# Layer 0's MLP of a two-layer decoder kernel: two stages over both halves of the tokens in place of one pass per half

## The chip, the cores and the metric

The kernel runs on one core of one Trainium2 chip, alone. The metric is device time in microseconds (us) of one execution; lower is better. TensorE (PE in the profile) multiplies, VectorE (DVE), ScalarE (ACT) and GpSimd (POOL) work on tiles of 128 partitions, and SyncE (SP) issues all DMAs between DRAM and SBUF from one queue, in program order. Each engine runs its own instructions in the order in which the program lists them. TensorE writes PSUM, which has here two wide buffers (pS, 1024 floats a partition) and four narrow ones (pB, 512).

## What is computed

A trunk of two decoder layers over 1024 tokens with 1024 features. Layer 0 has an attention over keys that an indexer selects (top 256 of the earlier ones), layer 1 a sliding window; both also read a fixed memory. Behind each attention stands a gated MLP with a causal convolution over three tokens. Cut to what matters here:

```python
D_MODEL, SEQ, DEPTH, D_FF, CONV_WIDTH = 1024, 1024, 2, 2816, 3

def conv_glu_ffn(h, w_up, conv_w, conv_b, w_down):
    S = h.shape[1]
    a, b = jnp.split(h @ w_up, 2, axis=-1)
    a_pad = jnp.pad(a, ((0, 0), (CONV_WIDTH - 1, 0), (0, 0)))
    a = sum(conv_w[j] * a_pad[:, j:j + S] for j in range(CONV_WIDTH)) + conv_b
    return (jax.nn.silu(a) * b) @ w_down

for i in range(DEPTH):
    h = rmsnorm(x, g_mix[i])
    mix, q_mem = mixer_a(h, ...) if i == 0 else mixer_b(h, ...)
    mem_o = memory_cross_attention(q_mem, mem_n, w_mem_kv[i])
    x = x + jnp.concatenate([mix, mem_o], axis=-1) @ w_out
    x = x + conv_glu_ffn(rmsnorm(x, g_ffn[i]), f_w_up[i], f_conv_w[i], f_conv_b[i], f_w_down[i])
return rmsnorm(x, g_final)
```

rmsnorm divides each token by the root of its mean square and multiplies each feature by a gain.

## The kernel before

**Tiles.** Activations lie with features on partitions and tokens along the row. Tokens are worked in two halves of 512 (`HT`). A half of x or h is four tiles, called pairs here, of 128 partitions x 1024: two blocks of 128 features, 512 tokens each. The 2816 inner features of the MLP are 22 tiles f of 128.

**Products.** Each fp32 operand is split into a rounded high part and a remainder, and `mm3` (L253) issues three matmuls for one product: high x high (L256), high x low (L257), low x high (L258). `proj` (L530) makes one tile of a projection by 8 blocks x 3 = 24 matmuls. `Weights` brings weights in the order of use: `LOAD` = 5 units are loaded ahead (512 KB each), `SPLIT` = 2 are split ahead: ScalarE casts the high part (L99) and POOL subtracts the remainder in two pieces of 512 (`rest`, L272, L279).

**What sets the order.** The program is written straight down for TensorE, and `tick(ns)` moves a clock by what the matmuls issued so far should take. Work beside it is written as generators (`add_bg`): each yields the time until its next step and is advanced by `tick`, at a rate of its own. So the place of each step among the instructions of VectorE, ScalarE and POOL is fixed when the program is built. Stores to DRAM are put off by 4000 ns of that clock, and a load from the same place flushes them first.

**Layer 0's MLP.** `run` (L1718) goes through the two halves: attention of the half (`run_a`), then `ffn` (L789) for that half alone. The attention's output step makes x; `prepare` takes its squares and splits x times gain without the scale of the norm, the raw h. `scale_of` sums the squares (folded on VectorE, L404 and L412, then summed by TensorE, L424), and spreads the scale as rb (transposes on TensorE, L443, a copy by ScalarE, L445). In `ffn`, `up(f)` projects raw h to the two parts a and b of tile f, `conv` multiplies a by rb (L801), does the convolution's middle tap on ScalarE (L802) and two more on VectorE (L803, L804), then Silu (L810) and the product with rb on POOL (L811); `gate` multiplies by b (L816) and splits the result (L820, POOL). After each two tiles `down` adds one chunk of the down projection of the chunk before to x (8 outputs in pairs, 48 matmuls into pS, four sums on VectorE, L867). Up and down weights are loaded once for each half.

**Beside it.** The selection of the 256 keys for the blocks 4 to 7 of 128 queries (`topk`, L1229) is a binary search over 32 bits: in each bit ScalarE counts by signs for blocks 6 and 7 (L1274), VectorE by comparisons for blocks 4 and 5 (L1254), and VectorE moves the candidates (L1265, L1267). It is held during the output step of half 0's attention (`late[1] = 0.0`), and goes on beside half 0's MLP once rb is there (`topk_on`), a step for each 2400 ns of the clock at rate 1.056. Then it builds the masks, and `begin_a` starts the second attention. Memory attention for half 1 follows in `memory`. Beside half 1's MLP run half 0's norm for layer 1 (`norm0`) and the memory's norm, keys and values (`mem_kv`).

**Layer 1's MLP** is built otherwise. `ffn_up` makes normalized h of both halves (`norm_apply`, L450: two products on VectorE for a pair, L469, a high part by ScalarE, L480, and a remainder on VectorE for pairs 0 and 2, L461, on POOL for the others), projects three tiles in the usual way, and the other 19 by seven products of blocks in place of eight (`group`), whose right factors are sums and differences of h blocks (`right_factors`, L892) and whose left factors come from `Weights._factor`. The gated results go to DRAM (`G_d`), and `ffn_down` reads them back chunk by chunk for both halves, with the down weights loaded once.

## Time and profile before

| | us |
|---|---|
| median of 3 runs (2630.15 to 2631.1) | 2630.22 |
| the profiled execution | 2624.22 |
| its span in the trace | 2622.4 |

The profile is one execution, so durations and sums are made against 2624.22 and then set against the median. By the page the engines were busy for 94% (TensorE), 65% (VectorE), 53% (POOL) and 46% (ScalarE) of the span. A busy TensorE is not TensorE at its peak: a matmul's records overlap the next one's, so the number of matmuls in a stretch without a gap is the better price. The stages lie, by the lines that end them, at: inputs of layer 0 to about 307 us, first attention to 530, half 0's MLP to 939, second attention to 1118, half 1's MLP to 1511, layer 1's attention to 1905, its up stage to 2353, its down stage to 2605.

### The profile page before, as it was taken

The page shows a single profiled execution, that of the slowest core. Times are in us where ns is not written, and L with a number is a line of the kernel's source. Part 1 is how long each engine was busy: PE and PEld are TensorE (multiplying, and loading weights), DVE is VectorE, ACT ScalarE, POOL GpSimd, SP SyncE. Part 2 cuts the span into 40 slices and gives each one's busy share as a digit, 9 for nine tenths or more (in the row PEclk, how much of TensorE's full clock was granted, in tenths as well). Part 3 has the DMA queues.
Part 4 walks back from the last instruction along what each step waited for, and adds up shares of the span by engine and source line. Part 5 has one row for each costly group of instructions (what it writes and reads, how often), then busy time and mean ns, then how long its engine had stood idle before and what let it go on. Part 6 is the DMA issues. An engine that isn't in the chain of part 4 may idle for free. (4 is left out here: it accounts for less than half of the span.)

```text
span 2622.4 us, 34006 instructions
## 1 busy us (share of the span) xinstructions
PE 2457.8 (94%) x11912; PEld 2053.0 (78%) x11912; DVE 1708.0 (65%) x2961; ACT 1207.9 (46%) x2270; POOL 1387.8 (53%) x1241
## 2 busy tenths in 40 slices
PE   7789978989998999999999989999989999999997
PEld 5678856878886888877888878878767888888886
DVE  7787788877688466665653353498786556564446
ACT  5355666655542555433333334588644444442003
POOL 5644223456665633365766665566656666664204
PEclk9899999999998999999999999999989999999999
DMA  5453343423322343322333345642254232348401
GB/s 202 148 172 120 127 159 135 149 78 97 98 87 91 126 155 107 113 97 82 105 127 97 99 115 187 213 139 88 81 193 137 104 122 97 123 170 329 142 16 65
DMA packets 121083, 333.83 MB, mean 127 GB/s; under 512 B 13008, under 2 KB 29904, under 8 KB 120912
## 3 DMA queue, kind: packets, MB, share of 16 engines
q1 hardware_dynamic: 120912, 331.66, 37.4%
q8 instruction: 94, 1.54, 0.2%
q14 instruction: 77, 0.63, 0.1%
HBM read 258.21 MB, written 73.40 MB: 126 GB/s over the span
## 5 line engine op out<-in xcount | busy, mean ns | idle before, releaser
L279 POOL TENSOR_TENSOR t<-t,t 128x512 fp32r<-128x512 f32 x829 | 1108.2, 1368 | 681.0 <-ACT t L99 273.6
L256 PE MATMUL pB<-t,t 128*128 128x512 f32 (+3 forms) x1824 | 682.1, 374 | 11.9 <-DVE t L781 4.1
L257 PE MATMUL pB<-t,t 128*128 128x512 f32 (+3 forms) x1824 | 678.8, 372 | 5.0 <-DVE t L461 2.4
L258 PE MATMUL pB<-t,t 128*128 128x512 f32 (+3 forms) x1824 | 678.3, 372 | 5.4 <-POOL t L279 5.4
L256 PE MATMUL pS<-t,t 128*128 128x512 f32 (+1 forms) x1460 | 573.8, 393 | 40.0 <-ACT t L99 19.1
L258 PE MATMUL pS<-t,t 128*128 128x512 f32 (+1 forms) x1460 | 568.5, 389 | 8.0 <-POOL t L279 7.8
L257 PE MATMUL pS<-t,t 128*128 128x512 f32 (+1 forms) x1460 | 568.0, 389 | 2.1 <-DVE t L512 2.1
L256 PEld LDWEIGHTS pB<-t,t 128*128 128x128 f32 (+1 forms) x1824 | 346.2, 190 | 72.8 <-DVE t L781 4.7
L258 PEld LDWEIGHTS pB<-t,t 128*128 128x128 f32 (+1 forms) x1824 | 345.9, 190 | 66.7 <-POOL t L279 6.7
L257 PEld LDWEIGHTS pB<-t,t 128*128 128x128 f32 (+1 forms) x1824 | 346.2, 190 | 64.7 <-DVE t L461 3.3
L256 PEld LDWEIGHTS pS<-t,t 128*128 128x128 f32 x1460 | 281.7, 193 | 100.4 <-ACT t L99 22.8
L99 ACT CAST t<-t 128x1024 fp32r<-128x1024 f32 x284 | 288.0, 1043 | 101.5 <-PE pS L258 44.1
L258 PEld LDWEIGHTS pS<-t,t 128*128 128x128 f32 x1460 | 281.0, 192 | 67.4 <-POOL t L279 12.1
L257 PEld LDWEIGHTS pS<-t,t 128*128 128x128 f32 x1460 | 281.8, 193 | 53.2 <-DVE t L512 2.5
L265 DVE TENSOR_TENSOR t<-pB,t 128x512 fp32r<-128x512 f32 (+3 forms) x248 | 149.8, 623 | 85.3 <-ACT t L264 82.7
L264 ACT CAST t<-pB 128x512 fp32r<-128x512 f32 (+3 forms) x248 | 125.7, 534 | 158.1 <-PE pB L258 96.2
L1055 DVE TENSOR_TENSOR t<-t,pS 128x1024 f32<-128x1024 f32 (+1 forms) x92 | 107.9, 1174 | 125.6 <-PE pS L258 125.5
L811 POOL TENSOR_TENSOR t<-t,t 128x512 f32<-128x512 f32 x44 | 57.5, 1306 | 161.6 <-ACT t L810 161.6
L867 DVE TENSOR_TENSOR t<-t,pS 128x1024 f32<-128x1024 f32 x88 | 106.8, 1217 | 53.0 <-PE pS L258 52.7
L1274 ACT ACTIVATE sign<-t,ti 128x1024 bf16<-128x1024 f32 (+1 forms) x96 | 96.5, 1005 | 60.5 <-DVE ti L1267 49.1
L1447 POOL TENSOR_SCALAR t<-t,st 128x128 f32<-128x128 f32 (+3 forms) x64 | 47.9, 750 | 141.3 <-DVE st L1446 88.0
L1222 DVE SCALAR_TENSOR_TENSOR t<-t,wtok,t 128x384 f32<-128x384 f32 (+5 forms) x90 | 97.0, 1077 | 24.5 <-ACT t L1217 20.7
(228 smaller groups left out, 3027.6 us busy)
## 6 DMA issues: line engine op xcount, KB each, us to landing
t<-in_up SPq DMA_DIRECT2D x138, 512.0 KB
t<-in_down SPq DMA_DIRECT2D x66, 512.0 KB
G_d<-t SPq DMA_DIRECT2D x44, 512.0 KB
t<-G_d SPq DMA_DIRECT2D x44, 512.0 KB
t<-in_a_in SPq DMA_DIRECT2D x34, 512.0 KB
t<-in_b_in SPq DMA_DIRECT2D x28, 512.0 KB
t<-in_a_out SPq DMA_DIRECT2D x20, 512.0 KB
t<-x_d SPq DMA_DIRECT2D x20, 512.0 KB
```

Source lines behind the costliest of these rows:

```text
L99: nc.scalar.copy(hi[:, :w], raw[:, :w])
L256: mm(out, a[0], b[0], start=start, stop=False, skip_group_check=again)
L257: mm(out, a[0], b[1], start=False, stop=False, skip_group_check=again)
L258: mm(out, a[1], b[0], start=False, stop=stop, skip_group_check=again)
L264: nc.scalar.copy(hi, src)
L265: nc.vector.tensor_tensor(lo, src, hi.bitcast(F32), op=OP.subtract)
L279: self.nc.gpsimd.tensor_tensor(lo[:, s], src[:, s], hi[:, s].bitcast(F32), op=OP.subtract)
L811: nc.gpsimd.tensor_tensor(v, v, rb[0], op=OP.mult)
L867: nc.vector.tensor_tensor(x[dp][:, :, t], x[dp][:, :, t], S, op=OP.add)
L1055: nc.vector.tensor_tensor(xp, xp, S, op=OP.add)
L1222: nc.vector.scalar_tensor_tensor(work[:, :n], tmp[:, :n], wv, work[:, :n], op0=OP.mult, op1=OP.add)
L1274: nc.scalar.activation(hits("sign")[:, :wide], self.work[blks[i]][:, :wide], AF.Sign, bias=cand[:, i:i + 1].bitcast(F32), accum_out=cnt[:, ...
```

## The change

Layer 0's MLP is built as layer 1's is. `ffn` is gone. After the first attention, `ffn_half` makes the up projection of tiles 0 to 16 for half 0 (tiles 0 and 1 from raw h, with rb as before, the others from normalized h0, as `finish` makes it); the second attention follows; `ffn_half` makes the same 17 tiles for half 1 (again two from raw h); `ffn_groups` makes tiles 17 to 21 for both halves by seven products, with factors from `right_factors`, which reads h0 back from DRAM and now also splits it again; and one `ffn_down` makes the down projection of both halves from `G_d`. The number of tiles done by halves is found while the program is built: as many as the second attention's beginning takes (`bt`).

The top-k runs on during the norm of half 0 and with pace 1200 in place of 2400 (`late_pace`). The second attention's beginning (`begin`) starts its key and value steps when the search has ended (the mark `found`), and its first units after the selection. Memory attention for half 1 now comes during the second attention. `norm0` and `mem_kv` run beside the down stage. x goes to DRAM after each attention and after the down stage.

The diff, cut; for layer 1 the same functions are called with other arguments:

```diff
-    def ffn(self, l, halves, fold=1, last=None, then=None):
...
-        nc = self.nc
-        G = {}
-        def conv(f, hf, a, rb):
...
-            nc.vector.tensor_tensor(v, a, rb[0], op=OP.mult)
-            nc.scalar.activation(u, v, AF.Identity, bias=cw[:, 3:4], scale=cw[:, 2:3])
-            nc.vector.scalar_tensor_tensor(u[:, 1:], v[:, :HT - 1], cw[:, 1:2], u[:, 1:], op0=OP.mult, op1=OP.add)
-            nc.vector.scalar_tensor_tensor(u[:, 2:], v[:, :HT - 2], cw[:, 0:1], u[:, 2:], op0=OP.mult, op1=OP.add)
...
-            nc.scalar.activation(v, u, AF.Silu)
-            nc.gpsimd.tensor_tensor(v, v, rb[0], op=OP.mult)
-            return u, v
...
-        def gate(f, hf, uv, b):
-            u, v = uv
-            nc.vector.tensor_tensor(u, v, b, op=OP.mult)
-            if f % 2 == 0:
-                G[hf, f // 2] = (self.t4(2, HT, dt=R32), self.t4(2, HT, dt=R32))
-            gh, gl = G[hf, f // 2]
-            nc.scalar.copy(gh[:, f % 2], u)
-            self.rest(gl[:, f % 2], u, gh[:, f % 2])
...
-            uvs = []
-            for i, (hf, x, h, rb, _) in enumerate(halves):
-                a = self.psB()
-                self.proj(a, wa, h)
-                if i == len(halves) - 1:
-                    wb = self.w.get(f"up{l}", NF + f)
-                uvs.append(conv(f, hf, a, rb))
-            for (hf, x, h, _, _), uv in zip(halves, uvs):
-                b = self.psB()
-                self.proj(b, wb, h)
-                gate(f, hf, uv, b)
...
-        ready = []
-        for f in range(NF):
-            up(f)
...
-            if f % 2:
-                if len(ready) >= fold and (last is None or f < NF - 1):
-                    down(ready[:fold], weights(ready[:fold]), halves)
-                    del ready[:fold]
...
-        if last is None:
-            while ready:
-                down(ready[:fold], weights(ready[:fold]), halves)
-                del ready[:fold]
...
-    def right_factors(self, hf1, out):
+    def right_factors(self, hf1, h1, out, h0=None):
...
+        def high(x):
+            hi, lo = self.t4(2, HT, dt=R32), self.t4(2, HT, dt=R32)
+            nc.scalar.copy(hi, x)
+            return x, hi, lo
+        def low(p, to):
+            x, hi, lo = p
+            tt(lo, x, hi.bitcast(F32), op=OP.subtract)
+            to.append((hi, lo))
...
-            for k, (x, y) in enumerate(((b12, b11), (b22, t[0]), (b22, b12), (b21, t[1]))):
-                tt(t[k], x, y, op=OP.subtract)
...
+            tt(t, b12, b11, op=OP.subtract)
+            yield 1400
+            p = high(t)
+            if h0 is not None:
+                q = high(b11)
+            tt(b12, b22, b12, op=OP.subtract)
+            yield 1400
+            low(p, out[0])
+            p = high(b12)
+            tt(t, b22, t, op=OP.subtract)
+            yield 1400
+            if h0 is not None:
+                low(q, h0)
+                q = high(b21)
                 yield 1400
-                if late:
...
+            low(p, out[2])
+            p = high(t)
+            yield 1400
+            if h0 is not None:
+                low(q, lower)
                 yield 1400
...
+            low(p, out[1])
+            tt(b21, b21, t, op=OP.subtract)
+            yield 1400
+            p = high(b21)
+            yield 1400
+            low(p, out[3])
...
+        if h0 is not None:
+            h0.extend(lower)
...
+    def keep(self, f, hf, u):
...
+        self.nc.scalar.copy(t[:, 0], u)
+        self.rest(t[:, 1], u, t[:, 0])
+        self.store("G", self.G_d[f][hf], t.bitcast(F32))
...
+    def ffn_half(self, l, fs, hf, h, rb=None, ahead=None):
...
+        for f in fs:
+            a, b = self.psB(), self.psB()
+            wa = self.w.get(name, f)
+            first = rb is not None and not rb
...
+            self.proj(a, wa, h)
+            uv = self.t4(2, HT)
+            u, v = uv[:, 0], uv[:, 1]
+            if first:
+                self.proj(b, wb, h)
+                while not rb:
+                    self.tick(100)
...
+            if rb:
+                nc.vector.tensor_tensor(v, a, rb[0], op=OP.mult)
+            self.conv(l, f, hf, v if rb else a, u)
+            if not first:
+                wb = self.w.get(name, NF + f)
...
+                self.proj(b, wb, h)
+            nc.scalar.activation(u, u, AF.Silu)
+            if rb:
+                nc.gpsimd.tensor_tensor(u, u, rb[0], op=OP.mult)
+            nc.vector.tensor_tensor(u, u, b, op=OP.mult)
+            self.keep(f, hf, u)
...
+    def ffn_groups(self, l, b11, b21, b22, B, fs, near_end):
...
+    def fetch(self, c, hf):
+        self.G[c, hf] = [self.t4(2, HT, dt=R32) for _ in range(2)]
+        for i in range(2):
+            self.load("G", self.G[c, hf][i].bitcast(F32), self.G_d[2 * c + i][hf])
...
+    def near_down(self, xs):
...
+    def ffn_down(self, l, xs, hooks, tail, last=None):
...
+        for c in range(nch - tail):
             us = weights(c)
             for hf in range(2):
-                if c + 1 + hf < nch:
-                    fetch(c + 1, hf)
+                self.fetch(c + 1, hf)
                 down(c, us, G.pop((c, hf)), hf)
...
+        us, cs = {}, range(nch - tail, nch)
+        order = [(c, hf) for hf in range(2) for c in cs]
+        for i, (c, hf) in enumerate(order):
+            if hf == 0:
+                us[c] = weights(c)
+            for e in order[i + 1:i + 3]:
+                if e not in G:
+                    self.fetch(*e)
+            down(c, us[c], G.pop((c, hf)), hf)
...
             if act:
                 step(bit, parts[-1])
-                yield pace
+                yield pace[0]
+        self.marks.add(("found", blks[0]))
...
+    def begin_a(self, att, selected=lambda: True):
...
         for s in kv_steps(0):
             yield s()
+        while not selected():
+            yield 500
...
-        def topk_on():
-            late[1] = 1.056
-            yield 0
...
-                def then():
-                    nonlocal att
-                    att = self.attn_a(1)
-                    bt.append(self.add_bg(self.spread(self.chain([lambda: iter([4000]), lambda: self.begin_a(att)]), 2950)))
...
-                def norm0():
-                    yield 55000
-                    x0 = self.load_x(self.x_d[0])
-                    yield from self.norm(x0, g[:, 1], hB0, 5000, 6000, 4000, True)
...
-                def mem_kv():
-                    yield 120000
-                    yield from self.mem_norm()
...
-                bt = [self.add_bg(mem_kv(), 0.8)]
-            self.ffn(0, [(hf, x, h, rb, hook)], then=then if hf == 0 else None)
...
+        def finish(x, sqs, rb, gain, h, wait, keep, dst):
...
+            yield from self.scale_of(sqs, rb, wait)
+            del sqs[:]
+            yield from self.norm_apply(rb[0], x, gain, 2, h, 2500, keep=keep)
+            yield from self.store_x(x, dst)
...
+        bn = self.add_bg(finish(x, sqs, rb, g[:, 3], h0, 1000, lambda i, t: self.store("hf", self.hf_d[i], t),
+                                self.x_d[0]))
...
+        late[1], late_pace[0] = 1.0, 1200
+        mem = self.mem_units(1)
...
+        def memory():
+            while late in self.bg:
+                yield 1000
+            self.load_qmem(1)
+            yield 9000
+            yield from self.whole(mem[0], 2200)
...
+        att = self.attn_a(1)
...
+        def begin():
+            while ("found", 4) not in self.marks:
+                yield 500
+            yield from self.spread(self.begin_a(att, lambda: late not in self.bg), 2950)
...
+        bm, bt = self.add_bg(memory()), self.add_bg(begin())
+        self.ffn_half(0, [0, 1], 0, raw, rb)
+        del raw[:]
+        while len(h0) < 4:
...
+        n_half = 2
+        while bt in self.bg or n_half < 3:
+            self.ffn_half(0, [n_half], 0, h0)
+            n_half += 1
...
+        bn = self.add_bg(finish(x, sqs, rb, g[:, 3], h1, 1000, lambda i, t: hf1.append(t), self.x_d[1]))
...
+        bT = self.add_bg(self.right_factors(hf1, h1, B, h0))
+        self.ffn_half(0, [0, 1], 1, raw, rb)
...
+        while len(h1) < 4:
+            self.tick(100)
+        self.ffn_half(0, list(range(2, n_half)), 1, h1, ahead=self.AHEAD)
...
+        b11, b21, b22 = h0[:2], h0[2:], h1[2:]
...
+        self.ffn_groups(0, b11, b21, b22, B, range(n_half, NF), self.near_down(xs))
...
+        bk = self.add_bg(mem_kv(), 0.8)
...
+        acc0, squares0 = self.squares(xs[0])
+        def norm0():
+            yield from self.norm_tail(acc0, xs[0], g[:, 1], hB0, 3000)
+            yield from self.store_x(xs[0], self.x_d[0])
...
+        self.ffn_down(0, xs, [hook0, hook1], 3)
...
-        self.ffn_down(1, xs, G, fetch, [last0, last1], 1)
+        self.ffn_down(1, xs, [last0, last1], 2, 1)
```

How this stands in the engines' order at three places. VectorE, after the scale of half 0's norm (the small `st` operations) and until the second tile's convolution, before; L801 to L804 and L816 are the convolution and product, L1265 to L1267 a step of the search, L1254 its scans:

```order
L801 TENSOR_TENSOR t_5290<-pB,t_5288 128x512
L803 SCALAR_TENSOR_TENSOR t_5290<-t_5290,conv 128x511
L804 SCALAR_TENSOR_TENSOR t_5290<-t_5290,conv 128x510
L816 TENSOR_TENSOR t_5290<-t_5290,pB 128x512
L1265 TENSOR_SCALAR ti<-tc 128x2
L1267 SCALAR_TENSOR_TENSOR ti<-ti 128x2
...
L801 TENSOR_TENSOR t_5341<-pB,t_5288 128x512
L803 SCALAR_TENSOR_TENSOR t_5341<-t_5341,conv 128x511
L804 SCALAR_TENSOR_TENSOR t_5341<-t_5341,conv 128x510
L1254 TENSOR_SCALAR hit,tc<-t_1911,ti 128x640
```

And after; L469 and L461 are the norm's products and remainder, L900, L863, L864 and L910 the convolution and product, L1212, L1223 and L1225 the search:

```order
L469 SCALAR_TENSOR_TENSOR t_5315<-t_3567,gains,t_5313 128x512 x2
L900 TENSOR_TENSOR t_5250<-pB,t_5313 128x512
L863 SCALAR_TENSOR_TENSOR t_5250<-t_5250,conv 128x511
L864 SCALAR_TENSOR_TENSOR t_5250<-t_5250,conv 128x510
L910 TENSOR_TENSOR t_5250<-t_5250,pB 128x512
L1223 TENSOR_SCALAR ti<-tc 128x2
...
L469 SCALAR_TENSOR_TENSOR t_5349<-t_3569,gains,t_5313 128x512 x2
L1212 TENSOR_SCALAR hit,tc<-t_1911,ti 128x640
L1212 TENSOR_SCALAR hit,tc<-t_2285,ti 128x768
L461 TENSOR_TENSOR t_5378<-t_5315,t_5376 128x1024
L469 SCALAR_TENSOR_TENSOR t_5380<-t_3571,gains,t_5313 128x512 x2
L900 TENSOR_TENSOR t_5383<-pB,t_5313 128x512
L863 SCALAR_TENSOR_TENSOR t_5383<-t_5383,conv 128x511
```

The norm's pairs (the fourth follows) now stand between the first tiles' convolutions and the scans.

ScalarE, one up tile in the middle of half 0's MLP, from the middle tap to the next tile's, before (beside 48 matmuls of the tile and 24 of a down chunk); L1274 is the search's sign scan, L99 the cast of a weight:

```order
L802 ACTIVATE t_5696<-t_5696,conv 128x512
L806 COPY prev_a<-t_5696 128x2
L810 ACTIVATE t_5696<-t_5696 128x512
L1274 ACTIVATE sign,tc<-t_2634,ti 128x1024
L820 CAST t_5736<-t_5696 128x512
L99 CAST t_5742<-t_5572 128x1024
L1274 ACTIVATE sign,tc<-t_3029,ti 128x1024
L99 CAST t_5780<-t_5647 128x1024
L802 ACTIVATE t_5785<-t_5785,conv 128x512
```

And after, beside the 48 matmuls alone; L1232 is the sign scan, L862, L866, L907 and L875 are the convolution's tap, the kept tokens, Silu and the split:

```order
L862 ACTIVATE t_5609<-pB,conv 128x512
L866 COPY prev_a<-pB 128x2
L99 CAST t_5616<-t_5460 128x1024
L1232 ACTIVATE sign,tc<-t_2634,ti 128x1024
L1232 ACTIVATE sign,tc<-t_3029,ti 128x1024
L907 ACTIVATE t_5609<-t_5609 128x512
L875 CAST t_5659<-t_5609 128x512
L99 CAST t_5666<-t_5511 128x1024
L1232 ACTIVATE sign,tc<-t_2634,ti 128x1024
L1232 ACTIVATE sign,tc<-t_3029,ti 128x1024
L862 ACTIVATE t_5708<-pB,conv 128x512
```

Four scans stand there in place of two, and the tap reads PSUM.

VectorE, after the scale of half 1's norm, before, the first tile and the beginning of the second:

```order
L801 TENSOR_TENSOR t_10298<-pB,t_10296 128x512
L803 SCALAR_TENSOR_TENSOR t_10298<-t_10298,conv 128x511
L804 SCALAR_TENSOR_TENSOR t_10298<-t_10298,conv 128x510
L808 SCALAR_TENSOR_TENSOR t_10298<-prev_a,conv,t_10298 128x1
L809 SCALAR_TENSOR_TENSOR t_10298<-prev_a,conv,t_10298 128x2
L816 TENSOR_TENSOR t_10298<-t_10298,pB 128x512
L801 TENSOR_TENSOR t_10346<-pB,t_10296 128x512
```

And after; L816, L821 and L804 are `right_factors`:

```order
L469 SCALAR_TENSOR_TENSOR t_9161<-t_7042,gains,t_9159 128x512 x2
L900 TENSOR_TENSOR t_9108<-pB,t_9159 128x512
...
L910 TENSOR_TENSOR t_9108<-t_9108,pB 128x512
L469 SCALAR_TENSOR_TENSOR t_9192<-t_7044,gains,t_9159 128x512 x2
L461 TENSOR_TENSOR t_9210<-t_9161,t_9208 128x1024
L469 SCALAR_TENSOR_TENSOR t_9212<-t_7046,gains,t_9159 128x512 x2
L900 TENSOR_TENSOR t_9215<-pB,t_9159 128x512
...
L469 SCALAR_TENSOR_TENSOR t_9246<-t_7048,gains,t_9159 128x512 x2
L461 TENSOR_TENSOR t_9263<-t_9212,t_9261 128x1024
L910 TENSOR_TENSOR t_9215<-t_9215,pB 128x512
L816 TENSOR_TENSOR t_9292<-t_9161,t_9081 128x1024
L821 TENSOR_TENSOR t_9161<-t_9212,t_9161 128x1024
```

The norm's four pairs and then the differences of h stand between the first tiles' operations.

## Rows read from the trace of the kernel before

**Rows 1.** The page, part 1: busy us (share of the span) xinstructions.

```profile
PE 2457.8 (94%) x11912; PEld 2053.0 (78%) x11912; DVE 1708.0 (65%) x2961; ACT 1207.9 (46%) x2270; POOL 1387.8 (53%) x1241
```

**Rows 2.** Stretches, TensorE: stretch, length, busy (xmatmul records), granted clock, DMA share, GB/s.

```profile
530.00:560.00 30.00, 25.12 (x104) 0.89 0.22 68
560.00:620.00 60.00, 57.48 (x248) 0.97 0.29 96
...
770.00:860.00 90.00, 78.07 (x327) 0.91 0.25 82
860.00:945.00 85.00, 81.04 (x401) 0.99 0.45 151
945.00:1118.00 173.00, 173.00 (x1081) 0.99 0.35 115
1118.00:1140.00 22.00, 18.16 (x73) 0.84 0.32 106
1140.00:1200.00 60.00, 58.24 (x256) 1.00 0.30 103
1945.00:2001.00 56.00, 49.26 (x204) 0.94 0.48 170
2005.00:2335.00 330.00, 330.00 (x1457) 1.00 0.32 113
2340.00:2360.00 20.00, 18.19 (x80) 1.00 0.73 270
2360.00:2575.00 215.00, 215.00 (x943) 0.99 0.40 149
```

**Rows 3.** Timeline, TensorE: start, us, engine, line, operation, [idle before <-releaser].

```profile
541.09 1.86 PE L424 MATMUL pS<-ones,t 128*128 128x1 f32 x8 [4.88 <-DVE t L412]
...
543.39 0.63 PE L257 MATMUL pB<-t,t 128*128 128x512 f32 x1
543.82 0.63 PE L258 MATMUL pB<-t,t 128*128 128x512 f32 x1
```

**Rows 4.** Waits of TensorE, 770 to 860: us in total, times, longest.

```profile
PE pS L258 <- POOL t L279: 5.3, 2, 3.1
PE pS L256 <- DVE ti L1301: 3.9, 1, 3.9
```

**Rows 5.** Timeline of ScalarE, 1888 to 1918.

```profile
1891.13 0.57 ACT L445 COPY t<-pB 128x512 f32<-128x512 f32 x1
```

**Rows 6.** Timeline of TensorE, 1908 to 1919.

```profile
1916.83 0.80 PE L258 MATMUL pB<-t,t 128*128 128x512 f32 x1 [0.99 <-POOL t L279]
```

**Rows 7.** Timeline of ScalarE, 1926 to 1962.

```profile
1927.55 0.58 ACT L445 COPY t<-pS 128x512 f32<-128x512 f32 x1 [4.25 <-PE pS L443]
```

**Rows 8.** Timeline of VectorE, 1926 to 1962.

```profile
1946.43 2.35 DVE L461 TENSOR_TENSOR t<-t,t 128x1024 fp32r<-128x1024 f32 x2
```

**Rows 9.** Lines, 530 to 1511: operation, shapes xcount, busy, mean ns, idle before.

```profile
L99 ACT CAST t<-t 128x1024 fp32r<-128x1024 f32 x146 | 147.0, 1045 | 0.1
...
L867 DVE TENSOR_TENSOR t<-t,pS 128x1024 f32<-128x1024 f32 x87 | 105.6, 1217 | 53.0 <-PE pS L258 52.7
...
L803 DVE SCALAR_TENSOR_TENSOR t<-t,conv 128x511 f32<-128x511 f32 x44 | 51.2, 1163 | 48.8 <-ACT t L802 48.8
L1274 ACT ACTIVATE sign<-t,ti 128x1024 bf16<-128x1024 f32 x42 | 48.0, 1144 | 21.3 <-DVE ti L1267 20.9
...
L1254 DVE TENSOR_SCALAR_CACHE_REDUCE hit<-t,ti 128x768 bf16<-128x768 f32 x22 | 22.2, 1008 | 0.3
```

**Rows 10.** Waits of ScalarE, 620 to 770.

```profile
ACT sign L1274 <- DVE ti L1267: 17.2, 5, 5.3
```

**Rows 11.** Lines, 2005 to 2335.

```profile
L944 DVE SCALAR_TENSOR_TENSOR t<-pB,conv,t 128x511 f32<-128x511 f32 x18 | 13.5, 750 | 51.3 <-ACT t L943 51.3
```

**Rows 12.** Timeline of VectorE, 1888 to 1918.

```profile
1891.74 1.41 DVE L469 SCALAR_TENSOR_TENSOR t<-t,gains,t 128x512 f32<-128x512 f32 x2 [1.60 <-ACT t L445]
...
1900.35 3.48 DVE L469 SCALAR_TENSOR_TENSOR t<-t,gains,t 128x512 f32<-128x512 f32 x2
```

274 lines of the change are left out of this document (104 added, 170 removed).

## The prediction

> **What bounds the kernel now.** I read the page's first part, then a table of stretches for TensorE alone, then what ended its waits, then the other engines in the stretches where it waits. TensorE is busy for 94% of the span [rows 1], so nothing but its own work and its waits can move the end. The reader should first fix the price of a matmul: in the calmest stretch of layer 1, 1457 matmuls fill 330.00 us without a gap, 0.2265 us each [rows 2]. A stretch's loss is then its length less 0.2265 for each full matmul (less for narrower ones). In layer 0's MLP of half 0 the losses sit in three places [rows 2]. At its start 530 to 560 loses about 8.9 us (104 records, 90 of them full matmuls) and 560 to 620 loses 3.8 (60 - 248 x 0.2265). From 770 to 860, where the top-k of blocks 4 to 7 is finished, it loses 18.4 (327 records, 306 of full width, 20 half). Half 1 loses 8.0 from 1118 to 1140 (73 records, 59 full) and about 2.5 from 1140 to 1200. The attention between them, 945 to 1118, has no idle time.
>
> Next, the waits. At 541.09 TensorE waits 4.88 us for VectorE's sum of squares, and the matmuls behind it start 0.43 us apart: the granted clock was at its lower level, 1.2 GHz, after the pause [rows 3]. So each longer pause costs more than its idle time. From 770 to 860 the longest waits are for POOL's remainders of weights, 5.3 us in two, and for a small VectorE operation of the selection, 3.9 in one [rows 4]. VectorE is late there, and what is late behind it is late on ScalarE, then POOL, then TensorE.
>
> **The change part by part.** *Matmuls.* A tile of the up projection by the usual way is 2 x 48 matmuls over both halves, by seven products 84. Five tiles save 5 x 12 = 60, and the built programs hold 11862 and 11802. 60 x 0.2265 = **-13.6 us**, all on the path. The down stage has as many matmuls as before.
>
> *Start of half 0.* Today the raw, unscaled h feeds all 22 tiles and the scale is applied to results, so TensorE never waits for a normalized h. Now tiles 0 and 1 are raw, and tile 2 reads h0, whose four pairs VectorE, ScalarE and POOL must first make. Layer 1 has the nearest rows twice. There the scale's copy to SBUF ends at 1891.13 + 0.57 = 1891.70 [rows 5], and TensorE gets the last remainder of the fourth pair at 1916.83 [rows 6]: 25.1 us. The second norm there has its copy end at 1928.13 [rows 7] and its last remainder at 1946.43 + 2.35 = 1948.8 [rows 8]: 20.6 us. What covers it? Behind the scale's transposes stand the 48 matmuls of tile 1, 10.9 us, which end some 10.1 us after the copy (I put the copy's end 0.8 us after the transposes). Tile 2's first product would end 5.4 later, at 15.5. If its last six matmuls begin at 25.1 and run at 0.43 each, it ends at 27.7: 12.1 us lost. In half 0 the top-k is no longer held back in this stretch, and the new VectorE order has four scans of about 1.0 us [rows 9] between the pairs. Some fall into waits, so I add 3: 28.1 for the last remainder, a loss of 15.1. The lower end is 7.6 (by 20.6). Two more scans stand in the fold that TensorE waits for at 541: +2.0. The 3.8 us of 560 to 620, a wait for the down sums' buffers, goes, since no down chunk follows. Together **+13.3**, from +4 to +20. While TensorE waits, behind the waiting product stand the rest of tile 2 and all later tiles; for those wait only their convolutions on ScalarE and VectorE.
>
> *The scan beside half 0.* Before, the 42 sign scans [rows 9] lie in some 210 us up to 770, one to 5 us; with pace 1200 in place of 2400 the new order puts four or five to each up tile of 10.9 us. 4.3 x 1.144 = 4.9 us, and two weight casts of 1.045 take 2.1 more [rows 9], before the tile's own three activations and the accumulators' reads. ScalarE comes close to full, in order, and weights are cast behind it. Lower end 0. Upper end 17.2, the time that its scans wait for VectorE's steps at the old pace [rows 10]. I take **+2**, since VectorE has less to do per tile.
>
> *The end of the top-k.* Before, an up tile and half a down chunk put a first tap of 1.163 and two sums of 1.217 beside it [rows 9]; now the tap reads PSUM at 0.750, as in layer 1 [rows 11], and the sums are in another stage. Per us of matmuls VectorE owes about 0.2 in place of 0.37, some 9 us less over the 55 us of the selection. But the key and value steps of the second attention, which came after it, now start inside it (some 7 us of evacuations and masked scores, my estimate), and the counts come at the faster pace. **-2**, from -16 (the whole loss but 2 goes) to +6.
>
> *Memory attention for half 1* moves from the end of half 0's MLP into the second attention, which has no idle to begin with; the stretch it leaves idled 4 us [rows 2]. **0**, from -3 to +5.
>
> *Start of half 1.* The first wait, 22 - 18.16 us, stays. The wait for h1 is new: **+12.1** by the same sum, 7.6 by the shorter norm. The differences of h follow on VectorE while tiles 2 to 7 run. The same generator costs layer 1 part of 56 - 203 x 0.2265 = 10.0 us [rows 2], but there it shares the stretch with three tiles only; I take +3, and 2.5 (1140 to 1200) goes. **+12.6**, from +2 to +20.
>
> *Down stage.* Layer 1's start loses 20 - 80 x 0.2265 = 1.9 and the rest 215 - 943 x 0.2265 = 1.4 [rows 2]. The memory norm and half 0's norm, which wait inside half 1's MLP today, wait inside this stage: 0. **+2**, from -2 to +6.
>
> *At nothing.* 44 stores and 44 loads of G and 32 fewer weight loads on SP: layer 1 runs the same pattern without a gap from 2005 to 2335 at a DMA share of 0.32 [rows 2]. The cover is that loads go five units ahead, 5 x 24 x 0.2265 = 27 us; a store that waits for a late remainder holds the loads behind it on SP, and beyond 27 us TensorE would wait. h and x go by 20 more DMAs on the same queue, under the same cover: each pair's store waits for VectorE's product of that pair. POOL loses 81 passes, VectorE its slower taps: neither is the bound.
>
> Sum: -13.6 + 13.3 + 2 - 2 + 0 + 12.6 + 2 = **+14.3 us**. The profiled execution took 2624.2 (span 2622.4, the rest around it), the median of the runs is 2630.2. Added to the median: **2644.5**.
>
> A rule to weigh it by. A pair of the norm's products on VectorE took 1.41 us at 1891.74 and 3.48 at 1900.35 [rows 12], and the tap fell from 1.163 [rows 9] to 0.750 when an input came from PSUM [rows 11]. The Trainium skill, SBUF — State Buffer, Who interferes with whom, has a VectorE instruction with two SBUF inputs contend with a GpSimd one that reads SBUF, as one lock on a shared port. By that rule the trace agrees, and the chain is short only while POOL rests. With all pairs at 1.41 the 25.1 would fall by about 5, and the sum by some 10, to 2634; with all at 3.48 the sum would rise as much.
>
> **The rivals.** *The norms are covered (faster).* Place: the third tile of each half. Price: 15.1 + 12.1. It decides by one point: if the last pair is usable 15.5 us after the scale's copy, TensorE loses nothing. For it: four pairs at 1.41 are only 5.6 us of work. Against it: 20.6 and 25.1 in the two cases seen, and tile 0's convolution stands between the pairs in the new order. 14.3 - 27.2 = -12.9: **2617**.
>
> *The selection is absorbed (no change).* An up tile's sums have four buffers and a tile takes two, so VectorE may be 16 us late before a buffer is missing, where a down sum gave about 3. Against it: the waits named were for weights, not only for buffers [rows 4]. The 18.4 goes whole, 16.4 more than in my sum: **2628**.
>
> *ScalarE becomes the bound (slower still).* If the scans at double pace wait as long as they did, the 17.2 comes in whole, 15 more than my sum: **2660**. For it: a load near full, in order. Against it: a scan waits for VectorE's step before it, and VectorE has the time now.
>
> That the products are not dropped is excluded by the count of the built program.
>
> **How the numbers follow.** Forecast 0.42 and ScalarE 0.14 are slower, 0.56. The selection absorbed 0.21 stands within 0.2%. The norms covered 0.16, and that with the selection absorbed as well 0.07 (2601), are faster, 0.23. About 0.2%, 5 us, is what a measurement of this kernel can tell from no change. The likeliest single time is 2644.5; its own range by the ends above is some 2628 to 2660. For 8 in 10 the range reaches over the covered norms and the bound on ScalarE: 2612 to 2662.
>
> **What would show it.** Right: about 10 to 15 us after the scale's copy in each half, TensorE waits in a product into pB for a cast, VectorE's or POOL's remainder of the norm (the lines that now stand in layer 1's waits), and the granted clock falls there. The five tiles of seven products run without a gap, and so does most of the down stage. The top-k's end still shows waits for POOL's weights. Wrong: tile 2 of either half starts on time; or half 0 shows 17 tiles without a gap; or weights wait for ScalarE's scans from tile 3 on; or the gap opens in the second attention, where I put nothing.

## The result, and the profile after

The changed kernel took 2666.12 us (median of 4 runs, 2660.57 to 2666.88) where the kernel before took 2630.66 beside it: a ratio of 1.0126, 95% interval 1.0109 to 1.0144. It is slower by 35.5 us; the forecast was 14 slower, with 2662 as the upper end. The profiled executions took 2660.57 and 2624.22, spans of 2658.8 and 2622.4, so the traces differ by 36.4 us, and the comparison by stretches is made between these two.

The page's first part for the changed kernel (the answer to [rows 1]):

```profile
PE 2461.5 (93%) x11852; PEld 2044.0 (77%) x11852; DVE 1746.0 (66%) x3001; ACT 1203.4 (45%) x2284; POOL 1290.0 (49%) x1160
```

TensorE has 60 instructions fewer and is busy 4 us longer. The stretches of TensorE after the change (columns as in [rows 2]):

```profile
540.00:560.00 20.00, 18.15 (x72) 0.83 0.07 27
560.00:580.00 20.00, 9.48 (x26) 0.66 0.61 210
...
620.00:700.00 80.00, 73.01 (x315) 0.98 0.53 180
700.00:820.00 120.00, 108.47 (x567) 0.97 0.38 131
820.00:940.00 120.00, 120.00 (x782) 1.00 0.36 113
...
980.00:1020.00 40.00, 33.49 (x125) 0.83 0.45 157
1020.00:1060.00 40.00, 33.62 (x131) 0.91 0.35 120
1060.00:1260.00 200.00, 200.00 (x884) 1.00 0.40 137
1260.00:1360.00 100.00, 92.15 (x449) 1.00 0.72 266
1970.00:2030.00 60.00, 48.78 (x193) 0.94 0.45 155
2030.00:2390.00 360.00, 360.00 (x1590) 1.00 0.33 115
```

The reader should look at four rows below full. From 560 to 580 only 26 matmuls run, and the granted clock falls to a mean of 0.66. From 620 to 700, 315 run (24 of half width) where 353 full ones fit. From 980 to 1060, 256 run where again 353 fit, and from 1970 to 2030, 193 where 265 fit. From 1060 to 1260, where the last tiles of half 1 and the five by seven products are made, nothing is lost: 884 matmuls, 0.2262 us each.

With the price of the prediction (0.2265 us for a full matmul, half for half width, a quarter for quarter width) the losses by stage are:

| stage | before, us lost | after | moved by | forecast |
|---|---|---|---|---|
| 60 matmuls fewer | | | -13.6 | -13.6 |
| start of half 0 (540 to 620) | 9.1 | 20.8 | +11.7 | +13.3 |
| the search beside half 0 (before 620 to 760, after 620 to 700) | 0.5 | 11.8 | +11.3 | +2 |
| end of the selection and first units of the attention (before 760 to 960, after 700 to 820) | 29.7 | 25.2 | -4.5 | -2 |
| the rest of the second attention (before 960 to 1100, after 820 to 940) | 17.2 | 14.8 | -2.4 | 0 |
| start of half 1 (before 1120 to 1200, after 960 to 1060) | 10.5 | 30.7 | +20.2 | +12.6 |
| the rest of layer 0 (before 1200 to 1520, after 1060 to 1540) | 12.5 | 17 | +4.5 | +2 |
| up stage of layer 1 (before 1920 to 2000, after 1950 to 2030) | 15.0 | 21.3 | +6.3 | not in the sum |

They add to +33.5; the rest of the traces' 36.4 is spread over the other stages. In the rows with attention in them a loss is not all idle time: from 820 to 940 TensorE is busy for 120.00 of 120 us, and the 14.8 are what narrow matmuls take beyond their share of the price.

### The profile page after: what moved, and what is told of

Read it like the earlier page. It is cut to its first block, busy times and chain, and to the rows that moved or that the text cites. A ratio compares the mean times of both kernels' runs of the same rounds, so it can differ in the third digit from the quotient of the medians.

```text
span 2658.8 us, 34054 instructions
## 1 busy us (share of the span) xinstructions
PE 2461.5 (93%) x11852; PEld 2044.0 (77%) x11852; DVE 1746.0 (66%) x3001; ACT 1203.4 (45%) x2284; POOL 1290.0 (49%) x1160
## 5 line engine op out<-in xcount | busy, mean ns | idle before, releaser
L279 POOL TENSOR_TENSOR t<-t,t 128x512 fp32r<-128x512 f32 (+1 forms) x788 | 1062.1, 1376 | 967.8 <-ACT t L99 393.5
L256 PE MATMUL pB<-t,t 128*128 128x512 f32 (+2 forms) x1744 | 658.6, 378 | 34.3 <-ACT t L480 14.8
L258 PE MATMUL pB<-t,t 128*128 128x512 f32 (+2 forms) x1744 | 654.8, 375 | 17.2 <-POOL t L279 17.2
L257 PE MATMUL pB<-t,t 128*128 128x512 f32 (+2 forms) x1744 | 654.9, 376 | 11.1 <-DVE t L461 5.5
L256 PE MATMUL pS<-t,t 128*128 128x512 f32 (+1 forms) x1520 | 593.8, 391 | 35.3 <-ACT t L99 16.8
L258 PE MATMUL pS<-t,t 128*128 128x512 f32 (+1 forms) x1520 | 588.7, 387 | 2.2 <-POOL t L279 2.0
L257 PE MATMUL pS<-t,t 128*128 128x512 f32 (+1 forms) x1520 | 588.6, 387 | 2.2 <-DVE t L512 2.2
L256 PEld LDWEIGHTS pB<-t,t 128*128 128x128 f32 (+1 forms) x1744 | 334.6, 192 | 99.1 <-ACT t L480 18.4
L258 PEld LDWEIGHTS pB<-t,t 128*128 128x128 f32 (+1 forms) x1744 | 334.1, 192 | 82.7 <-POOL t L279 25.3
L257 PEld LDWEIGHTS pB<-t,t 128*128 128x128 f32 (+1 forms) x1744 | 334.3, 192 | 72.9 <-POOL t L279 9.1
L256 PEld LDWEIGHTS pS<-t,t 128*128 128x128 f32 x1520 | 291.2, 192 | 95.6 <-ACT t L99 19.8
L1011 DVE TENSOR_TENSOR t<-t,pS 128x1024 f32<-128x1024 f32 (+1 forms) x180 | 214.9, 1196 | 219.0 <-PE pS L258 217.3
L258 PEld LDWEIGHTS pS<-t,t 128*128 128x128 f32 x1520 | 290.5, 191 | 62.2 <-POOL t L279 4.6
L257 PEld LDWEIGHTS pS<-t,t 128*128 128x128 f32 x1520 | 291.2, 192 | 55.2 <-DVE t L512 2.6
L99 ACT CAST t<-t 128x1024 fp32r<-128x1024 f32 x242 | 248.5, 1044 | 171.5 <-PE pS L258 118.3
L863 DVE SCALAR_TENSOR_TENSOR t<-pB,conv,t 128x511 f32<-128x511 f32 x60 | 44.9, 748 | 145.0 <-ACT t L862 145.0
L105 ACT CAST t<-t 128x512 fp32r<-128x512 f32 x168 | 100.8, 616 | 60.6 <-DVE t L122 33.4
L1232 ACT ACTIVATE sign<-t,ti 128x1024 bf16<-128x1024 f32 (+1 forms) x96 | 96.7, 1007 | 55.4 <-DVE ti L1225 37.4
```

The lines of the kernel that those rows point to most:

```text
L99: nc.scalar.copy(hi[:, :w], raw[:, :w])
L105: nc.scalar.copy(hl[:, 0], src)
L256: mm(out, a[0], b[0], start=start, stop=False, skip_group_check=again)
L257: mm(out, a[0], b[1], start=False, stop=False, skip_group_check=again)
L258: mm(out, a[1], b[0], start=False, stop=stop, skip_group_check=again)
L279: self.nc.gpsimd.tensor_tensor(lo[:, s], src[:, s], hi[:, s].bitcast(F32), op=OP.subtract)
```

## The experiments

All run the changed kernel with an edit; gains are against its 2666.1 us. The kernel before, run beside each of the four sets, took 2630.6, 2627.7, 2627.2 and 2627.8 us (beside the changed kernel 2630.7), so a gain of some 4 us or less cannot be told from none by the times alone.

**Shorter scans, shorter counts, both.** The edits, in order (the third is both together):

```diff
-                    nc.scalar.activation(hits("sign")[:, :wide], self.work[blks[i]][:, :wide], AF.Sign,
+                    w = 128 if pace[0] == 1200 else wide
+                    nc.scalar.activation(hits("sign")[:, :w], self.work[blks[i]][:, :w], AF.Sign,
```

```diff
-        def count(i, op):
-            nc.vector.tensor_scalar(hits("hit")[:, :(blks[i] + 1) * 128], wks[i], cand[:, i:i + 1].bitcast(F32), 0.0,
+        def count(i, op, w=None):
+            w = w or (blks[i] + 1) * 128
+            nc.vector.tensor_scalar(hits("hit")[:, :w], wks[i][:, :w], cand[:, i:i + 1].bitcast(F32), 0.0,
...
-                    count(k, OP.is_ge)
+                    count(k, OP.is_ge, 128 if pace[0] == 1200 else None)
```

> From half 0's MLP on, the search's sign scans on ScalarE read 128 columns in place of 1024, so its counts (and with them the selected keys) are not the reference's; all else stands as in the changed kernel. Between 620 and 760 us the changed kernel loses 18 us against 0.3 before. Theory A, scan and step wait for each other in turn: ScalarE (59 of 80 us busy from 600 to 680) and VectorE (66 of 80) are both below full, and a sign scan, a step on VectorE and the next scan form a chain of some 3.3 us for each scan. 42 scans shorter by about 0.85 us give 36 us back to that chain, the loss falls to at most 4, and the time to about 2652. Theory B, ScalarE is full by itself: the same here; the run with short counts tells them apart. Theory C, weights come late for another reason (stores of the gated results on SP ahead of weight loads): the loss stays within 4 of 18, the time near 2665.

> From half 0's MLP on, VectorE's own counts for blocks 4 and 5 read 128 columns in place of 640 and 768, so the selection is not the reference's; ScalarE's scans are whole. Theory A (scans and steps wait for each other): 42 counts shorter by about 0.7 us give 29 us back to the chain, the loss from 620 to 760 falls from 18 to at most 6, the time to about 2654. Theory B (ScalarE is full by itself): the loss stays at 15 or more and the time above 2661.

> From half 0's MLP on, both the sign scans and VectorE's counts of the search read 128 columns, so the selection is not the reference's. Signs alone gave 7 us, counts alone nothing. Theory B (ScalarE's scans, in order ahead of the weights' casts): counts give nothing beside short signs either, the loss from 620 to 700 stays at 4 and the time at 2658 to 2660. Theory A (scans and counts wait for each other in turn, and the longer of both decides): with both short the loss from 620 to 700 goes to under 1.5, the time to 2653 to 2656. In both the loss from 700 to 820, where the candidates are counted and the masks built, is the 25 us of the changed kernel less at most 5.

Measured 2658.9, 2663.7 and 2651.1 us. TensorE from 620 to 700 with short scans, with short counts, and with both:

```profile
620.00:700.00 80.00, 77.64 (x349) 1.00 0.53 181
```

```profile
620.00:700.00 80.00, 72.27 (x308) 0.98 0.53 180
```

```profile
620.00:700.00 80.00, 80.00 (x366) 1.00 0.55 187
```

The losses there are 4.1, 13.4 and 0.3 us (24 of the records are of half width), against 11.8. Short counts alone give nothing, short scans two thirds, both all of it. So the 11.3 us are the search's, and neither engine's part of it stands alone: the scans decide, and once they are short the counts do. Neither engine was full (in the changed kernel ScalarE was busy for 52 and VectorE for 67 of these 80 us). From 700 to 820 the losses stay at 25 to 27 in all three: counting candidates and building masks cost what they did.

**Weights split earlier; remainders on VectorE.** One unit more of lead, or the remainders of half 0's gated results taken off POOL:

```diff
-                self.w.SPLIT = Weights.SPLIT
+                self.w.SPLIT = 3 if l == 0 and hf == 0 else Weights.SPLIT
...
+        self.w.SPLIT = Weights.SPLIT
```

```diff
-    def keep(self, f, hf, u):
+    def keep(self, f, hf, u, l=1):
...
-        self.rest(t[:, 1], u, t[:, 0])
+        if l == 0 and hf == 0:
+            self.nc.vector.tensor_tensor(t[:, 1], u, t[:, 0].bitcast(F32), op=OP.subtract)
+        else:
+            self.rest(t[:, 1], u, t[:, 0])
...
-            self.keep(f, hf, u)
+            self.keep(f, hf, u, l)
```

> In half 0's MLP weights are split three units ahead in place of two, after the first tile; the scans stay. With the sign scans cut to 128 columns the loss between 620 and 740 fell from 12 to 10 us only in part, with VectorE's counts cut not at all. Theory D, lateness and not fullness: a weight's cast stands on ScalarE behind the split of the tile before, which waits for that tile's last product on VectorE, and the scans and steps push it some us past the moment of need; ScalarE itself has 27% of its time free. One unit more of lead is 5.4 us, so the loss from 620 to 760 falls from 18 to under 5 and the time from 2666 to about 2653. Theory B, ScalarE and VectorE lack throughput for scans at this pace: the lead is used up after a few tiles, the loss stays above 12, the time above 2660.

> In half 0 the remainder of the gated results is taken by VectorE in one pass in place of POOL in two. While POOL works on such a pair and a weight's, the search's small steps on VectorE take 1.1 to 1.2 us each, and 0.16 at other times, in the changed kernel; ScalarE's next scan waits for them up to 1.9 us. Theory P, POOL's passes stretch the steps and these hold the scans: the steps' mean falls by half, the loss from 620 to 700 from 12 to about 6, the time to about 2660. Theory B (ScalarE's own scans): VectorE's additional 0.7 us to a tile change nothing or cost some us: 2664 to 2670.

Measured 2664.5 and 2672.9 us. With the lead, 17.8 us are lost from 620 to 760 against 18.3: the waits for weights fall from 10.4 to 3.8, and waits come up for tiles that are read out late (3.2 us for prev_a, 2.2 for the product). So more lead does not help: what it gives is lost again within the stretch. The second run does not clear POOL. It takes away one of POOL's five passes for a tile (the expectation says two), and the two kinds of small steps of the search on VectorE fell from means of 630 and 377 ns to 468 and 344 from 600 to 700, some 4 us in all, while the remainders cost VectorE 5.5 us there. The loss from 620 to 700 rose to 16, and how much of it POOL's passes make stays open.

**A slower pace.**

```diff
-        late[1], late_pace[0] = 1.0, 1200
+        late[1], late_pace[0] = 1.0, 1400
```

> The search goes on beside half 0's MLP at pace 1400 in place of 1200; 19 tiles by halves and 3 by seven products, 24 matmuls more. Theory B, an up tile's 10.9 us hold too little of ScalarE for its scans at pace 1200: with 3.8 scans to a tile in place of 4.4 the loss while the search runs (12 us from 620 to 700 in the changed kernel, 4 with the scans cut short) falls to about 4, the 24 matmuls cost 5.4: the time falls by about 3, to 2663. Theory C, the losses are not the scans': the loss stays at 11 or 12 and the time rises by 5.4, to 2671.

2667.0 us. From 620 to 700 7.1 us are lost in place of 11.8, and two more tiles by halves cost 24 matmuls, 5.4 us. The two cancel: what the slower pace spares TensorE in waits is paid in products.

**The start of the halves.** A third raw tile; the search held during the norm; a shorter chain:

```diff
-        self.ffn_half(0, [0, 1], 0, raw, rb)
+        self.ffn_half(0, [0, 1, 2], 0, raw, rb)
...
-        n_half = 2
-        while bt in self.bg or n_half < 3:
+        n_half = 3
+        while bt in self.bg:
...
-        self.ffn_half(0, [0, 1], 1, raw, rb)
+        self.ffn_half(0, [0, 1, 2], 1, raw, rb)
...
-        self.ffn_half(0, list(range(2, n_half)), 1, h1, ahead=self.AHEAD)
+        self.ffn_half(0, list(range(3, n_half)), 1, h1, ahead=self.AHEAD)
```

```diff
-        late[1], late_pace[0] = 1.0, 1200
...
+        late[1], late_pace[0] = 1.0, 1200
```

```diff
-                nc.gpsimd.tensor_tensor(u, u, rb[0], op=OP.mult)
-            nc.vector.tensor_tensor(u, u, b, op=OP.mult)
+                nc.vector.tensor_tensor(v, b, rb[0], op=OP.mult)
+            nc.vector.tensor_tensor(u, u, v if rb else b, op=OP.mult)
...
-            yield from self.norm_apply(rb[0], x, gain, 2, h, 2500, keep=keep)
+            yield from self.norm_apply(rb[0], x, gain, 2, h, 1200, keep=keep)
```

> Three tiles from raw h in place of two at the start of both halves; matmuls as many as in the changed kernel. Theory A: the waits for normalized h (14 us lost from 560 to 580, some 10 from 980 to 1000) are its latency, 28 us from the scale's copy to the last remainder, and a third raw tile covers 10.9 us more: the losses fall to about 4 and 0, and the time by 15 to 20, to about 2649. Theory E: the third raw tile's scale, taps and product stand on VectorE and POOL between the pairs and delay them by as much: the time stays within 5 of 2666.

> The search of the top-k stands still until h0 is whole, as it did before the change during the norm, and goes on at pace 1200 after. The selection then ends later, so that 19 tiles are made by halves and 3 by seven products: 24 matmuls more, 5.4 us. Theory A: four scans and their steps cost the chain of the norm some 4 us and the fold before it 0.5 to 2; the loss from 540 to 580 falls from 20 to about 15, and the whole gets no better: 2664 to 2669. Theory F, the scans are what makes the norm late: the loss falls under 8, the time to about 2658.

> For the two raw tiles of each half the scale is multiplied into b on VectorE while Silu runs, in place of POOL's product after it, and the norm's pairs are put 1200 in place of 2500 ns apart in the program. In the changed kernel VectorE waits 3.5 us for POOL in front of the second pair, and the last remainder is there 28 us after the scale's copy. Theory A: the chain is VectorE's order; it shortens by 6 to 8 us in each half, the losses from 540 to 580 and from 980 to 1020 fall from 20 to 13 and from 18 to 11, the time to about 2652. Theory E: the weights of the next tiles come late in place of it, as they did with a third raw tile, and the time stays within 4 of 2666.

Measured 2678.3, 2666.9 and 2661.9 us. The third raw tile made it 12 us slower, which neither theory had. The waits of TensorE with it, from 560 to 620 and from 990 to 1060 (us in total, times, longest):

```profile
PE pB L256 <- ACT t L99: 9.1, 3, 5.3
PE pB L258 <- POOL t L279: 2.1, 3, 0.9
```

```profile
PE pB L256 <- ACT t L99: 13.2, 4, 6.7
```

No wait for the norm's casts (L480) is left, as theory A has it. But weights come late in their place. By the program's order a weight's cast stands on ScalarE behind the split of the tile before, that behind a product on VectorE, and VectorE has the norm, the raw tiles' extra scale and the counts to do; no run takes these apart. With the search held, 540 to 580 loses 18.7 us against 19.8, but in that trace the work stands 1.5 us later. Counted between the same two matmuls, the stretch is 2.8 us shorter, and the waits for the normalized h are 8.5 us in place of 11.6. So the search makes some 3 us of that wait, near theory A's 4, and not most of it. The shorter chain gains 4.3 in all, nearer to theory E and at the edge of what can be told. It loses 14.9 from 540 to 580, 5 less, of which weights take 3.4 back from 580 to 620; in half 1 it gains nothing while right_factors follows at once (24.1 against 22.7 from 980 to 1060).

**right_factors, spread in layer 0, and as it was in layer 1.** In the first only the yields change (1400 to 4200 when h0 is given); in the second the kernel before's function stands beside the new one under the name right_old:

```diff
-                yield 1400
+                yield gap
...
-        bT = self.add_bg(self.right_factors(hf1, h1, B))
+        bT = self.add_bg(self.right_old(hf1, B))
```

> In layer 0 alone, right_factors yields 4200 in place of 1400 between its steps, so that the differences and splits of h spread over three times as many tiles of half 1. Theory A: the waits for weights between 1020 and 1060 (10.8 us lost) come from VectorE, ScalarE and POOL being held by these steps; they go to under 3, and the time falls by some 8 to 2658. Theory B: they come from stores queued on SP ahead of the weight loads, and stay: 2665. The wait for h1 before (17.6 us lost from 980 to 1020 and the first wait) is the same in both.

> In layer 1 alone, right_factors is the kernel before's (four differences of h in another order, begun when hf1 holds three pairs rather than when h1 does). Between the norms of layer 1's first half and the end, the changed kernel takes 728.8 us where the kernel before took 722.2. Theory A: the new order of these steps makes the difference, all of it between 1970 and 2030; it goes back to 722 or 723, and the time to about 2660. Theory B: the three tiles' new loop or the stores make it, and the 728.8 stays within 2.

Measured 2652.5 and 2658.1 us: 13.6 and 8.0 less. TensorE from 1020 to 1060 with the steps spread, and from 1970 to 2030 with the old function; then the kernel before in its like stretch, 30 us earlier:

```profile
1020.00:1060.00 40.00, 40.00 (x178) 1.00 0.52 184
```

```profile
1970.00:2030.00 60.00, 53.51 (x223) 0.94 0.50 179
```

```profile
1940.00:2000.00 60.00, 53.26 (x221) 0.94 0.48 171
```

The 10.8 us from 1020 to 1060 are gone, and 1970 to 2030 holds 223 matmuls in place of 193, as the kernel before did (221). Both losses were these steps. The first run's trace is only 5.4 us shorter than the changed kernel's, where the medians differ by 13.6; the traces are of executions of 2655.2 and 2660.6 us, off their medians in opposite ways. Matmul for matmul, the stretch from 1020 to 1060 is 10.7 us shorter, and the rest 5.3 longer.

**Memory keys later.**

```diff
-            yield 5000
+            yield 20000
...
-        bk = self.add_bg(mem_kv(), 0.8)
+        bk = self.add_bg(mem_kv(), 0.5)
```

> The memory's norm, keys and values begin 20000 in place of 5000 ns into layer 0's down stage and go at rate 0.5 in place of 0.8. Theory A: the waits for sums of the down stage (10 us lost from 1260 to 1360, where layer 1's down stage loses 2 to 4 in its first 100 us) come from the memory norm's work on VectorE, and spread out they go to about 4: the time falls by 5, to about 2661. Theory G: they come from the first G loads or the squares and are there without it: the same time.

2663.5 us, 2.6 less and within the runs' scatter. From 1260 to 1360 6.3 us are lost in place of 10.4, and 4.3 more from 1360 to 1420: the waits for the down sums move with the memory's norm, so it makes them, but they are moved rather than gone.

**All mends together**, at pace 1400 and 1200, and with more of the search in the first attention:

```diff
-        late, late_pace = [], [2400]
+        late, late_pace = [], [1800]
```

> All at once: right_factors spread in layer 0 (13.6 less alone), the kernel before's in layer 1 (8.0 less alone), memory keys later and slower (2.6 less alone), the shorter start of both halves (7 each by theory A) and pace 1400 (3 less). If the gains add, 2666 - 13.6 - 8.0 - 2.6 - 14 - 3 = 2625, some 5 under the kernel before. If the start's gain is lost to late weights, 2639. If pace 1400 costs its matmuls in full, 8 more in both.

> The version of all mends (right_factors spread in layer 0, the kernel before's in layer 1, memory keys later and slower, the shorter start) with pace 1200 in place of 1400: 17 tiles by halves, 24 matmuls fewer. If the two paces are as even as they were alone (2666.1 and 2667.0), 2635 to 2637. If the scans at pace 1200 cost more now that the start leaves less slack, 2639 to 2642.

> The version of all mends at pace 1400, with the search at pace 1800 in place of 2400 already beside the first attention, so that fewer of its 21 last bits are left for half 0's MLP: 17 tiles by halves again at pace 1400. From 440 to 540 the first attention keeps VectorE 88% and ScalarE 65% busy and loses 7 us. Theory H, the attention has room for a third more scans: its loss stays within 2 and the time falls by the 24 matmuls, 5.4, to about 2631. Theory I, VectorE has no room there: the loss moves into the attention, and the time is 2636 or more.

Measured 2636.0, 2637.7 and 2640.4 us. The single gains add (2666.1 - 13.6 - 8.0 - 2.6 - 4.3 + 0.8 = 2638.4), but all three are still slower than the kernel before: 1.0033 (1.0020 to 1.0046), 1.0035 (1.0021 to 1.0048) and 1.0048 (1.0031 to 1.0064). The search beside half 0 still costs 11.8 us from 620 to 700 at pace 1200. More of it in the first attention saves 24 matmuls against the first version and is 4.4 us slower still: it moves the loss. TensorE from 500 to 560 in that run and in the changed kernel:

```profile
500.00:560.00 60.00, 50.03 (x225) 0.88 0.21 69
```

```profile
500.00:560.00 60.00, 53.57 (x240) 0.94 0.12 43
```

No version beat the kernel before.

## Why the prediction was wrong

The direction, the sign of most terms and the waits for normalized h held. The sum was 21 us short, by three steps: the search beside half 0 (9 us), the differences of h in half 1 (8), and layer 1, which was left out (6).

*Start of half 0: right in size, in part by luck.* Timelines of ScalarE, TensorE, VectorE and POOL (start, us, engine, line, operation, idle before), which answer [rows 5 to 8]:

```profile
548.07 0.59 ACT L445 COPY t<-pS 128x512 f32<-128x512 f32 x1 [2.08 <-PE pS L443]
...
570.41 1.15 ACT L1232 ACTIVATE sign<-t,ti 128x1024 bf16<-128x1024 f32 x1 [2.99 <-DVE ti L1225]
...
571.56 1.03 ACT L480 CAST t<-t 128x1024 fp32r<-128x1024 f32 x1
```

```profile
561.38 0.49 PE L256 MATMUL pB<-t,t 128*128 128x512 f32 x1 [2.44 <-ACT t L480]
563.67 0.50 PE L257 MATMUL pB<-t,t 128*128 128x512 f32 x1 [1.79 <-DVE t L461]
...
572.64 0.80 PE L256 MATMUL pB<-t,t 128*128 128x512 f32 x1 [6.79 <-ACT t L480]
573.99 0.79 PE L257 MATMUL pB<-t,t 128*128 128x512 f32 x1 [0.56 <-POOL t L279]
```

```profile
556.60 0.69 DVE L910 TENSOR_TENSOR t<-t,pB 128x512 f32<-128x512 f32 x1 [3.47 <-POOL t L909]
...
557.75 2.44 DVE L469 SCALAR_TENSOR_TENSOR t<-t,gains,t 128x512 f32<-128x512 f32 x2
```

```profile
575.69 3.02 POOL L279 TENSOR_TENSOR t<-t,t 128x512 fp32r<-128x512 f32 x2 [0.51 <-ACT t L480]
```

The copy ends at 548.66 and the last remainder at 578.71: 30.1 us, where the prediction had 28.1 (the 28 us of some expectations end with the first of this row's two passes). TensorE waits in tile 2 for the casts, the remainders on VectorE and POOL, and its clock falls, as the forecast's list had it, and the whole term came to 11.7 where 13.3 was taken.

The way there was another. TensorE's last wait, at 573.99, is for the second pair, not the fourth, whose remainder is there in time. The second pair's products end at 560.19, but its cast begins at 571.56, because two operations that wait for VectorE stand before it on ScalarE: tile 1's middle tap, 4.25 us for a product, and a scan, 2.99 us for a step of the search. And two errors of the prediction cancel in part. Its 25.1 us from layer 1 end at 1916.83, in a wait of L258, which takes a weight's remainder; the remainder of h is the second factor of L257, and the fourth pair's was taken earlier, in this row of the kernel before:

```profile
1914.62 0.50 PE L257 MATMUL pB<-t,t 128*128 128x512 f32 x1 [1.09 <-POOL t L279]
```

That is 22.9 us after the copy. What the prediction did not see is the 3.47 us in which VectorE stands at 556.60 before tile 0's product, waiting for POOL, with the norm's second pair behind it. Half 1, which has no scans, shows the same: 3.41 us of that wait, and 26.4 us from the copy to the last remainder. For the fold at 541 TensorE waits 5.4 us in place of 4.9, not 2 more. The rule on VectorE's pairs says little here: three of the four took 1.4 us, and the chain was longer than in layer 1. Its upper side was also mis-added, as the pairs in layer 1 took 1.41, 2.88, 3.48 and 2.88 us, so that all at 3.48 add some 6.5 us over both halves, not 10.

*The search beside half 0: the term was mis-sized, the first step that failed.* The prediction took 2 from 0 to 17.2, "since VectorE has less to do per tile"; 11.3 were measured. A tile may give VectorE less, but it is now 48 matmuls where it shared 72 with a down chunk, and the search beside it is twice as dense. Per us VectorE had more to do. All engines from 620 to 700, before and after (busy us of PE, PEld, DVE, ACT, POOL; then the clock, DMA share and GB/s):

```profile
620.00:700.00 80.00, 80.00 (x354) 65.92 (x353) 58.39 (x97) 43.73 (x66) 52.33 (x41) 1.00 0.28 91
```

```profile
620.00:700.00 80.00, 73.01 (x315) 57.20 (x314) 66.57 (x130) 52.08 (x85) 42.12 (x34) 0.98 0.53 180
```

One turn of the chain, in rows of ScalarE, then of VectorE, of POOL and of TensorE:

```profile
617.26 1.14 ACT L1232 ACTIVATE sign<-t,ti 128x1024 bf16<-128x1024 f32 x1
...
620.36 1.15 ACT L1232 ACTIVATE sign<-t,ti 128x1024 bf16<-128x1024 f32 x1 [1.86 <-DVE ti L1225]
...
623.88 0.16 ACT L866 COPY prev_a<-pB 128x2 f32<-128x2 f32 x1 [1.60 <-DVE t L864]
623.94 1.05 ACT L99 CAST t<-t 128x1024 fp32r<-128x1024 f32 x1
```

```profile
616.66 1.14 DVE L1223 TENSOR_SCALAR ti<-tc 128x2 int32<-128x2 f32 x1
617.83 1.19 DVE L1225 SCALAR_TENSOR_TENSOR ti<-ti 128x2 int32<-128x2 int32 x1
618.95 0.15 DVE L1223 TENSOR_SCALAR ti<-tc 128x2 int32<-128x2 f32 x1
619.14 1.13 DVE L1225 SCALAR_TENSOR_TENSOR ti<-ti 128x2 int32<-128x2 int32 x1
```

```profile
616.48 3.77 POOL L279 TENSOR_TENSOR t<-t,t 128x512 fp32r<-128x512 f32 x3 [3.66 <-ACT t L875]
```

```profile
625.04 0.50 PE L256 MATMUL pB<-t,t 128*128 128x512 f32 x1 [0.68 <-ACT t L99]
```

A scan ends at 618.40, the next begins at 620.36, because three of the four small steps took over 1.1 us beside POOL's passes. Behind that scan stand the tile's middle tap, then a wait of 1.60 us, then the weight's cast, and TensorE gets that weight at 625.04. The wait of 1.60 us is easily overlooked. It is ScalarE's copy of the tokens that are kept for half 1 (L866), which stands idle until VectorE's second tap is done; before the change that copy read SBUF and never waited. It is ScalarE's longest wait from 620 to 700, 12.5 us in 7, against 5.3 in 3 for the search's steps. No run moved it, so its share is not shown. With both scans and counts short it still waits 9.7 us and nothing is lost, so it does not make the loss alone. Nor does the pace alone; TensorE in two parts of the stretch:

```profile
620.00:650.00 30.00, 25.00 (x97) 0.94 0.35 117
650.00:670.00 20.00, 20.00 (x90) 1.00 0.34 124
```

Some 8 us are lost in the first part and nothing in the second, at the same pace. What begins the lateness there is not shown. The rival "ScalarE becomes the bound" named the place, with 15 us more than the sum where 9 more were measured, though not all of the mechanism: ScalarE was 65% busy, VectorE 83%, and both the scans and the counts had to be short for the loss to go.

*The end of the top-k: right in sign.* -4.5 where -2 was taken, within its ends; the rival that it goes whole fell, as three runs left its 25 us where they were.

*Start of half 1: the wait right, the differences of h mis-sized.* The waits of TensorE from 980 to 1060:

```profile
PE pB L256 <- ACT t L99: 3.6, 2, 2.7
PE pB L258 <- POOL t L279: 2.8, 3, 2.1
PE pB L256 <- ACT t L480: 2.5, 2, 2.2
PE pB L257 <- POOL t L279: 2.5, 1, 2.5
PE pB L257 <- DVE t L461: 1.4, 1, 1.4
```

The last three lines are the waits for h1, all before 1020; 11.9 us are lost from 980 to 1020, where 12.1 was taken for them. The 3 us for the differences of h were 10.8, lost from 1020 to 1060 in waits for weights (the first two lines). The table's +20.2 is these two less the 2.5 of the kernel before. This is the second step that failed. The prediction said that layer 1 shares the stretch with three tiles only and so took a third of it; but the steps stand 1400 ns apart in both layers, and so are as dense on VectorE and ScalarE whether three tiles follow or fifteen. The run with the steps spread shows it: at 4200 ns nothing is lost there.

*Layer 1: left out, the third step.* The diff rewrites right_factors for both layers, and the prediction put nothing for layer 1, without a reason. It cost 6.3 us, shown by the old function there. Which of its differences does it (the later beginning, the reuse of tiles that makes a difference wait for a cast) was not separated.

*Down stage:* +4.5 in the rest of layer 0, within its ends; waits that move with the memory's norm are there, where the prediction put 0. *At nothing:* the G stores and loads cost nothing that a run showed: with short scans and counts, 620 to 700 is without a gap at a DMA share of 0.55.

The rival of covered norms fell at both halves, as TensorE waited in the third tile of each.

*The range* reached to one rival at a time. The search at 11, half 1 at the upper end of its term (20) and layer 1's 6 came together, and that lies above 2662.
